# Key tiles on a fixed eight-tick cycle, log decays masked by GpSimd and exponentiated by ScalarE, gate steps one engine hop a tick

## Chip, cores and metric

The kernel runs on one core of a Trainium2 chip. The metric is the device time of one execution in microseconds, the median of several runs. A profile comes from one further execution. Engines: TensorE (PE; its weight loads are PEld), VectorE (DVE), ScalarE (ACT), GpSimd (POOL), and SyncE (SP), whose queue here issues DMAs only. Each engine works through its own queue in order and waits for the others by semaphores.

## The reference

One residual block on x of 1024 tokens by 1024 channels, all in float32. What matters here is the gated delta-rule branch (eight heads of 128 channels), which shares its input projection with a gated linear-attention branch and is followed by an output product and a squared-ReLU MLP.

```python
h = rms_norm(x, pre_mix_w) * (1.0 + scale1) + shift1        # scale1, shift1 from silu(c) @ ada_w
proj = h @ w_in                                             # d_qkv, d_beta, d_a and more are slices of it
d_qkv = silu(causal_short_conv(d_qkv, gdn_conv_w))          # four taps along the tokens
d_k = l2_norm(d_k)                                          # per token and head
beta = sigmoid(d_beta)
g = -exp(gdn_a_log) * softplus(d_a + gdn_dt_bias)
gc = cumsum(g)                                              # within a chunk of tokens
decay_mat = exp(where(causal, gc[:, None] - gc[None, :], -inf))
a_mat = where(strict, (k * beta) @ k.T * decay_mat, 0)
# then (a_mat + 1) is solved against the right-hand sides, and a scan over chunks follows
```

So for each head the key stage must give the keys, the sums of their squares, the decay matrices, and the products k k^T times the decay matrices.

## The kernel before

**Products in parts.** A float32 product is made of three passes in a reduced float32 format: each operand is split into a high part (hH, wH) and a rest (hL, wL). One dense product of 128 output channels for all 1024 tokens (`dense_b`, line 459) goes through eight contraction steps of six matmuls. After each step `tick()` advances a clock by one and runs what an agenda holds for it: `at(dt, fn)` (line 346) enters a function some ticks ahead, and `run_due` issues it behind the last matmul in TensorE's order. A tick decides only the place in the queues: VectorE, ScalarE, GpSimd and SP run their part as soon as their own queue and their inputs let them.

**Order.** `InOrder` (line 27) wraps an engine. While its flag `strict` is set, every instruction is placed behind the one before it on that engine, so the order is that of the program text and the agenda. The flag is set from line 135 to line 1333 (the end of the last key tile's dense product); from there a planner orders instructions by its own estimate and can also put later instructions between the strict ones where it thinks that an engine is free.

**Prologue** (lines 138 to 338). The tokens are loaded, squared (`x_sq`, ScalarE), scaled (`x_scale`, VectorE) and transposed in two groups (`x_tr` on TensorE, copied out of PSUM by `x_copy`). The conditioning vector's products are accumulated in four parts (`ada_pe`, `ada_out`), summed over partitions by `ada_fin` (TensorE) and turned into two columns per part, scale `am1` and shift `sh1`, by `ada_cols` (VectorE). `high(p)` makes two tiles of hH from the transposed tokens and these columns on ScalarE, `low(p)` the tiles of hL on VectorE.

**First tiles** (`first_tiles`, line 474). Two key heads and the 32 columns for low-rank gate, beta and a (weights `raw_lba`, split into `wS`) are computed together while the parts of the conditioning vector arrive. PSUM of a key head goes through `key_copy` (ScalarE: copy with the last tap), `key_tap` three times (VectorE), `key_tanh` (ScalarE) and `key_silu` (VectorE).

**Key stage** (lines 1312 to 1332). Tick 0 is the start of the first of six dense products, one for each of heads 2 to 7, which end at ticks 8, 16, ... 48. In their ticks run:

- the gates (`gates_small`, line 563): rows of beta and a go to DRAM and back into 64 partitions, then functions g6 to g11 at ticks 6 to 11 compute beta, the softplus, its running sum gc and derived columns. g8 writes gc to DRAM, g9 has GpSimd load it back, spread over 128 partitions, for heads 0 to 3 (`load_decay`, tile `Dk[h]`, named gr in the trace), g10 transposes three tiles on TensorE, g11 copies them to columns (gcC, betaC, ksC, beC);
- for each head `key_head` (line 709) with the ticks given in its call: transposes of the key in two halves, squares with sums (ktok), decays (eight instructions on VectorE per head: the row of gc less a column of gc, plus `negmask`, which is -1e30 above the diagonal), one exponential over the whole tile on ScalarE, Gram products in two halves on TensorE, their product with the decays (`times`, tile a0) on VectorE, and five stores. The tiles of gc have four buffers (tag hd), those of PSUM for these steps four (`pat`), and two for dense products (`pmt`).

For heads 4 to 7 the transposes stand at ticks 6 and 7 after the end of the head's dense product, and the silu at 5.

**After it** the agenda goes on during the two branch-gate products: `key_norms` (norms of the keys, two transposes of columns on TensorE), then `solve`, 64 steps on VectorE. `smask` is a mask tile that GpSimd fills at line 1345.

Of the kernel before, what the change touches and what calls it, by code (L numbers as in the profile page):

```python
# [50 lines left out]
def block_kernel(ctx: ExitStack, tc: tile.TileContext, x, c, ada_w, ada_b, pre_mix_w, post_mix_w,  # L51
# [253 lines left out]
    r1 = x_root(1)  # L305
    x_scale(1, r1)

# [166 lines left out]
    def first_tiles():  # L474
        wS = t4((128, 8, 64), F32R, "wS", "wt")
# [3 lines left out]
        A.copy(wS[:, :, 0:32], raw_lba)  # L479
        V.tensor_tensor(wS[:, :, 32:64], raw_lba, wS[:, :, 0:32].bitcast(F32), ALU.subtract)  # L480
# [61 lines left out]
        t1 = key_tanh(y1)  # L542
        key_silu(y1, t1)
# [13 lines left out]
    gcC = cp.tile([128, 64], F32, name="gcC")  # L557
# [5 lines left out]
    def gates_small(sb):  # L563
# [11 lines left out]
        def g6():  # L575
            A.activation(beta, bt, AF.Tanh, scale=0.5)
            V.tensor_scalar(beta, beta, 0.5, 0.5, ALU.mult, ALU.add)
            V.tensor_scalar(at_, at_, dtb, None, ALU.add)
            A.activation(e, at_, AF.Abs)
            A.activation(e, e, AF.Exp, scale=-1.0)  # L580
            A.activation(al, al, AF.Exp)

        def g7():
            V.tensor_scalar(u, e, 1.0, None, ALU.add)
            A.activation(l, u, AF.Ln)
            V.tensor_scalar(w, u, -1.0, None, ALU.add)
            V.tensor_tensor(w, e, w, ALU.subtract)
            V.reciprocal(u, u)
            V.tensor_mul(w, w, u)
# [30 lines left out]
        for i, fn in enumerate((g6, g7, g8, g9, g10, g11)):  # L620
            at(6 + i, fn)
# [15 lines left out]
        for t, fn in ((36, lr_high), (37, lr_low), (44, wlr_split)):  # L637
# [65 lines left out]
    Dk = {}  # L703
# [5 lines left out]
    def key_head(h, k, on, tr, decay, ex, gram):  # L709
# [1344 lines left out]
```

## Time and profile before

| | us |
|---|---|
| median of 3 runs | 1948.54 (1947.93 to 1952.42) |
| the profiled execution | 1951.02 |
| its span, first to last instruction | 1949.0 |
| TensorE busy in the span | 1910.4 |
| VectorE busy | 1343.5 |
| ScalarE busy | 811.4 |
| GpSimd busy | 141.4 |
| mean granted TensorE clock | 0.993 |

The profile gives a page of totals, groups of instructions, waits with what ended them, the chain of work that ended last, a timeline in order of time, and busy times in chosen stretches. Times in it are from the span's start. A row of the timeline reads: start, duration, engine, line, operation, output<-input, shapes, count, and in brackets the idle time before it and what ended it. All lines are L38, that of the helper that wraps the engines; tiles are told by name: cv is a key head between copy and silu, si a tanh, s the gates' tile, gr the decays, a the Gram products, wH and wL weight parts, pm and pa PSUM. The granted clock is that which TensorE's throttle let through, 1.00 being full.

### The profile page before, as it was taken

What the parts mean: (1) busy time and instruction counts of PE and PEld (TensorE: products, weight loads), DVE (VectorE), ACT (ScalarE), POOL (GpSimd) and SP (SyncE); (2) the same over time, 40 slices, a digit from 0 to 9 for tenths busy, and PEclk for the clock granted to TensorE, in tenths of its full rate; (3) what the DMA queues carried; (4) which work ended last, traced back from release to release, by engine and by line L of the source; (5) the groups of instructions that cost most, each with busy time, mean ns of one, the idle gap of its engine ahead of it and who ended that gap; (6) DMA issues with size and microseconds to landing.
All of it is one profiled execution on the core that took longest, in us unless ns stands there. A gap on an engine that the chain in (4) does not pass through costs nothing.

```text
span 1949.0 us, 25799 instructions
## 1 busy us (share of the span) xinstructions
PE 1910.4 (98%) x9873; PEld 1603.1 (82%) x9873; DVE 1343.5 (69%) x2427; ACT 811.4 (42%) x1477; POOL 141.4 (7%) x124
## 2 busy tenths in 40 slices
PE   6999999999999999999999999999999999999998
PEld 4687888889899888888887888888888888888886
DVE  5677699458768566766666244667578876787887
ACT  4545323342342334444445231357644446433333
POOL 1100100210101100000000110000012210000001
PEclk9999999999999999999999999999999999999999
DMA  9286423323122434444456986245656677452525
GB/s 326 71 254 208 140 98 111 127 66 109 53 78 66 142 107 137 128 129 129 129 190 162 226 191 145 87 130 167 219 197 229 226 237 267 143 205 74 196 97 98
DMA packets 213321, 296.96 MB, mean 152 GB/s; under 512 B 32687, under 2 KB 151710, under 8 KB 213198
## 3 DMA queue, kind: packets, MB, share of 16 engines
q1 hardware_dynamic: 188398, 259.38, 40.9%
q0 software_dynamic: 19280, 16.73, 5.5%
q10 hardware_dynamic: 5520, 19.21, 2.5%
q8 instruction: 77, 1.26, 0.3%
q14 instruction: 46, 0.38, 0.1%
HBM read 220.14 MB, written 75.15 MB: 152 GB/s over the span
## 4 chain that ended last, share of the span: by engine, by line
PE 91%; DMA 1%; DVE 1%; issue 1%; ACT 1%; POOL 0%; SPq 0%; DVEq 0%; POOLq 0%
PE pm L38 60%; PE pa L38 31%; DMA wL<-in_w_branch_gla_dram 1%; DVE cv L38 0%; ACT ktok L38 0%; DMA a_d<-a 0%; DVE gr L38 0%; ACT L38 0%; DVE ya L38 0%; DMA kt_d<-ktok 0%; DVE wL L38 0%; DVE lrS L38 0%; DVE rt L38 0%; ACT cv L38 0%; ACT wH L38 0%
## 5 line engine op out<-in xcount | busy, mean ns | idle before, releaser
L38 PE MATMUL pm<-hH,wH 128*128 128x512 f32 x992 | 327.2, 411 | 0.3 <-DVE cv L38 0.3
L38 PE MATMUL pm<-hL,wH 128*128 128x512 f32 x992 | 309.4, 393 | 0.0
L38 PE MATMUL pm<-hH,wL 128*128 128x512 f32 x992 | 308.0, 392 | 0.0
L38 PEld LDWEIGHTS pm<-hL,wH 128*128 128x128 f32 x992 | 187.2, 189 | 41.6
L38 PEld LDWEIGHTS pm<-hH,wL 128*128 128x128 f32 x992 | 187.0, 189 | 41.7
L38 PE MATMUL pa<-w,yH 128*128 128x512 f32 x688 | 212.0, 389 | 0.0
L38 ACT CAST wH<-raw 128x1024 fp32r<-128x1024 f32 x94 | 98.3, 1050 | 272.4 <-PE pm L38 197.4
L38 PEld LDWEIGHTS pm<-hH,wH 128*128 128x128 f32 x992 | 170.4, 191 | 22.6 <-issue 0.4
L38 DVE TENSOR_TENSOR w<-raw,w 128x512 fp32r<-128x512 f32 (+1 forms) x144 | 125.7, 877 | 49.1 <-ACT w L38 48.4
L38 PEld LDWEIGHTS pa<-w,yH 128*128 128x128 f32 x688 | 129.0, 188 | 27.3 <-DVE ya L38 0.4
L38 ACT CAST w<-raw 128x512 fp32r<-128x512 f32 (+1 forms) x142 | 97.2, 706 | 88.4 <-DVE raw L38 79.3
L38 PE MATMUL pa<-w,yL 128*128 128x512 f32 x344 | 133.8, 389 | 0.0
L38 PE MATMUL pa<-oB,w 128*128 128x512 f32 x480 | 111.4, 390 | 0.0
L38 DVE TENSOR_TENSOR wL<-raw,wH 128x1024 fp32r<-128x1024 f32 x78 | 94.7, 1218 | 22.0 <-ACT wH L38 11.9
L38 PEld LDWEIGHTS pa<-oB,w 128*128 128x128 f32 x480 | 89.7, 188 | 18.6 <-DVE w L38 0.2
L38 DVE SCALAR_TENSOR_TENSOR cv<-pm,ccol,cv 128x1023 f32<-128x1023 f32 (+2 forms) x72 | 92.0, 1277 | 13.9 <-ACT cv L38 12.9
L38 PE MATMUL pm<-oT,w 128*128 128x512 f32 x384 | 90.8, 389 | 0.0
L38 PE MATMUL pa<-oT,w 128*128 128x512 f32 x384 | 90.8, 389 | 0.0
L38 DVE TENSOR_TENSOR ya<-pa,ya 128x512 f32<-128x512 f32 x82 | 55.8, 688 | 43.7 <-PE pa L38 43.7
L38 PEld LDWEIGHTS pa<-oT,w 128*128 128x128 f32 x384 | 72.1, 188 | 15.0
L38 PEld LDWEIGHTS pm<-oT,w 128*128 128x128 f32 x384 | 72.1, 188 | 15.0
L38 PE MATMUL pm<-oH,wH 128*128 128x512 f32 x256 | 82.0, 402 | 0.9 <-DVE si L38 0.9
(339 smaller groups left out, 3665.4 us busy)
## 6 DMA issues: line engine op xcount, KB each, us to landing
yL<-y_d SPq DMA_DIRECT2D x53, 512.0 KB, 6.2
raw<-in_mlp_w_dram SPq DMA_DIRECT2D x23, 1024.0 KB
raw<-in_w_in_dram SPq DMA_DIRECT2D x20, 1024.0 KB, 7.4
raw<-in_w_in_dram SPq DMA_DIRECT2D x32, 512.0 KB, 4.1
araw<-in_ada_w_dram SPq DMA_DIRECT2D x32, 512.0 KB, 4.3
raw<-in_mlp_w_dram SPq DMA_DIRECT2D x18, 512.0 KB, 5.9
araw<-in_ada_w_dram SPq DMA_DIRECT2D x32, 256.0 KB, 6.8
sg_d<-sig ACTq DMA_DIRECT2D x16, 512.0 KB, 4.5
```

The source lines that it names most:

```text
L38: r = fn(*args, **kw)
```

## The change

In the prologue the split of the small weights `wS` moves from `first_tiles` to before and after the second `x_scale`; the conditioning sums of part 0 and their columns move between the transposes of the second group; one PSUM copy moves from ScalarE to VectorE. In `first_tiles` the tanh of head 0 is issued ahead of the copy of head 1, and the tanh and silu of head 1 go to ticks 2 and 3 of the key stage.

The gates' functions are cut anew, so that each holds about one engine's step after another's, and start at tick 3. The loads of gc for heads 0 to 3 are followed on GpSimd by `mask_decay`, which writes -1e30 above the diagonal of each tile; `negmask` goes. `decays` is now eight exponentials on ScalarE with the column of -gc (`gcN`, made by ScalarE from PSUM) as bias, in the place of eight instructions on VectorE and one exponential. `key_head` takes pairs of ticks for the two halves of each step, in a cycle of eight ticks from head 4 on: transposes at 9 and 13 after the dense product's end, squares a tick later, decays at 11 and 13, Gram products at 13 and 14, their products at 14 and 15.

```diff
     r1 = x_root(1)
+    wS = t4((128, 8, 64), F32R, "wS", "wt")
+    A.copy(wS[:, :, 0:32], raw_lba)
     x_scale(1, r1)
+    V.tensor_tensor(wS[:, :, 32:64], raw_lba, wS[:, :, 0:32].bitcast(F32), ALU.subtract)
...
     for i in range(4, 8):
+        if i == 6:
+            ada_fin(0)
+            ada_cols(0)
         x_tr(i, (4, 5, 0, 1, 2, 3) if i < 7 else (0, 1, 4, 5, 2, 3))
-    for d, E in ((0, A), (1, V), (4, A), (5, V), (2, A)):
+    for d, E in ((0, A), (1, V), (4, A), (5, V), (2, V)):
         x_copy(E, 1, d)
-    ada_fin(0)
-    ada_cols(0)
     banks[6:8] = [pat(), pat()]
     for i in range(4, 8):
         x_tr(i, (6, 7))
+    high(0)
     for d in (3, 6, 7):
         x_copy(V, 1, d)
-    high(0)
...
     def first_tiles():
-        wS = t4((128, 8, 64), F32R, "wS", "wt")
...
-        A.copy(wS[:, :, 0:32], raw_lba)
-        V.tensor_tensor(wS[:, :, 32:64], raw_lba, wS[:, :, 0:32].bitcast(F32), ALU.subtract)
...
-        y1 = key_copy(1, pk[1])
         for s_ in (1, 2, 3):
             key_tap(0, pk[0], y0, s_)
+        t0 = key_tanh(y0)
+        y1 = key_copy(1, pk[1])
         V.tensor_copy(sb[0:32], sb2[32:64])
         V.tensor_add(sb[0:32], sb[0:32], sb2[0:32])
-        t0 = key_tanh(y0)
         key_silu(y0, t0)
         for s_ in (1, 2, 3):
             key_tap(1, pk[1], y1, s_)
-        t1 = key_tanh(y1)
-        key_silu(y1, t1)
...
-        def g6():
+        def g3():
             A.activation(beta, bt, AF.Tanh, scale=0.5)
-            V.tensor_scalar(beta, beta, 0.5, 0.5, ALU.mult, ALU.add)
             V.tensor_scalar(at_, at_, dtb, None, ALU.add)
+
+        def g4():
             A.activation(e, at_, AF.Abs)
             A.activation(e, e, AF.Exp, scale=-1.0)
             A.activation(al, al, AF.Exp)
-
-        def g7():
+            V.tensor_scalar(beta, beta, 0.5, 0.5, ALU.mult, ALU.add)
+
+        def g5():
             V.tensor_scalar(u, e, 1.0, None, ALU.add)
-            A.activation(l, u, AF.Ln)
             V.tensor_scalar(w, u, -1.0, None, ALU.add)
             V.tensor_tensor(w, e, w, ALU.subtract)
-            V.reciprocal(u, u)
-            V.tensor_mul(w, w, u)
+
+        def g6():
+            A.activation(l, u, AF.Ln)
+            V.reciprocal(e, u)
+            V.tensor_mul(w, w, e)
...
         def g9():
+            for h in range(4):
+                load_decay(h)
+            for h in range(4):
+                mask_decay(h)
+
+        def g10():
             A.activation(kse, kse, AF.Exp)
             A.activation(dec, gc[:, 127:128], AF.Exp)
-            for h in range(4):
-                load_decay(h)
...
-            G.dma_start(decB, dec_d.partition_broadcast(128))
-
-        def g10():
+
+        def g12():
             z["ps"] = pat()
...
-        def g11():
-            for i, dst in ((1, gcC), (0, betaC), (2, ksC)):
+        def g13():
+            A.activation(gcN, z["ps"][:, 64:128], AF.Copy, scale=-1.0)
+            A.activation(beC, z["ps"][:, 64:128], AF.Exp)
+            for i, dst in ((0, betaC), (2, ksC)):
                 V.tensor_copy(dst, z["ps"][:, i * 64:(i + 1) * 64])
-            A.activation(beC, gcC, AF.Exp)
...
-        for i, fn in enumerate((g6, g7, g8, g9, g10, g11)):
-            at(6 + i, fn)
+        for t, fn in ((3, g3), (4, g4), (5, g5), (6, g6), (8, g8), (9, g9), (10, g10), (12, g12), (13, g13),
+                      (24, lambda: G.dma_start(decB, dec_d.partition_broadcast(128)))):
+            at(t, fn)
...
-        for t, fn in ((36, lr_high), (37, lr_low), (44, wlr_split)):
+        for t, fn in ((32, lr_high), (40, lr_low), (48, wlr_split)):
...
+    def mask_decay(h):
+        G.affine_select(out=r3(Dk[h]), in_=r3(Dk[h]), compare_op=ALU.is_ge, fill=-1e30, base=0,
+                        pattern=[[0, 8], [1, 128]], channel_multiplier=-1)
...
             for t in range(hf * 4, hf * 4 + 4):
-                V.scalar_tensor_tensor(gr[:, t * 128:(t + 1) * 128], gr[:, t * 128:(t + 1) * 128],
-                                       gcC[:, h * 8 + t:h * 8 + t + 1], negmask, ALU.subtract, ALU.add)
+                A.activation(gr[:, t * 128:(t + 1) * 128], gr[:, t * 128:(t + 1) * 128], AF.Exp,
+                             bias=gcN[:, h * 8 + t:h * 8 + t + 1])
...
-        on(tr, lambda: DMA.dma_start(kT_d[h], k))
-        on(tr, lambda: transposes(0))
-        on(tr + 1, lambda: squares(0))
-        on(tr + 1, lambda: transposes(1))
-        on(tr + (5 if h > 1 else 2), lambda: squares(1))
-        on(tr + 7, lambda: DMA.dma_start(kt_d[h], z["tok"]))
+        on(tr[0], lambda: DMA.dma_start(kT_d[h], k))
         for hf in range(2):
-            on(decay + hf, lambda hf=hf: decays(hf))
-            on(gram + hf, lambda hf=hf: grams(hf))
-            on(gram + hf + 1, lambda hf=hf: times(hf))
-        on(ex, lambda: A.activation(Dk[h], Dk[h], AF.Exp))
-        on(ex + 1, lambda: DMA.dma_start(Dt_d[h], Dk[h]))
-        on(gram + 3, spill)
+            on(tr[hf], lambda hf=hf: transposes(hf))
+            on(sq[hf], lambda hf=hf: squares(hf))
+            on(ex[hf], lambda hf=hf: decays(hf))
+            on(gram[hf], lambda hf=hf: grams(hf))
+            on(times_[hf], lambda hf=hf: times(hf))
+        on(sq[1] + 1, lambda: DMA.dma_start(kt_d[h], z["tok"]))
+        on(ex[1] + 1, lambda: DMA.dma_start(Dt_d[h], Dk[h]))
+        on(times_[1] + 1, spill)
         if h > 3:
-            on(decay - 6, lambda: load_decay(h))
+            on(ex[0] - 8, lambda: load_decay(h))
+            on(ex[0] - 3, lambda: mask_decay(h))
...
-    key_head(0, keys[0], on, 3, 13, 15, 17)
-    key_head(1, keys[1], on, 7, 15, 18, 19)
+    z1 = {}
+    on(2, lambda: z1.__setitem__("t", key_tanh(keys[1])))
+    on(3, lambda: key_silu(keys[1], z1["t"]))
+    key_head(0, keys[0], on, (1, 4), (3, 5), (19, 21), (21, 22), (22, 23))
+    key_head(1, keys[1], on, (6, 10), (7, 11), (23, 23), (23, 23), (24, 24))
...
-        key_head(h, y, on, e_ + 6, *{2: (20, 23, 25), 3: (23, 26, 30)}.get(h, (e_ + 6, e_ + 13, e_ + 14)))
+        ends = {2: ((27, 29), (29, 30), (30, 31)), 3: ((31, 31), (31, 31), (32, 32))}.get(
+            h, ((e_ + 11, e_ + 13), (e_ + 13, e_ + 14), (e_ + 14, e_ + 15)))
+        key_head(h, y, on, (e_ + 9, e_ + 13), (e_ + 10, e_ + 14), *ends)
...
-    at(14, key_norms)
-    at(26, lambda: next(sv))
-    due = 34.0
+    at(17, key_norms)
+    at(29, lambda: next(sv))
+    due = 37.0
```

More of the change, by code (lines that the diff above doesn't have):

```diff
@@ L556, in block_kernel @@
     nbrC = cp.tile([128, 64], F32, name="nbrC")
-    gcC = cp.tile([128, 64], F32, name="gcC")
+    gcN = cp.tile([128, 64], F32, name="gcN")
     ksC = cp.tile([128, 64], F32, name="ksC")
@@ L707, in load_decay, with key_head @@
         G.dma_start(Dk[h], gc_d[h].partition_broadcast(128))
-    def key_head(h, k, on, tr, decay, ex, gram):
+    def mask_decay(h):
+        G.affine_select(out=r3(Dk[h]), in_=r3(Dk[h]), compare_op=ALU.is_ge, fill=-1e30, base=0,
+                        pattern=[[0, 8], [1, 128]], channel_multiplier=-1)
+    def key_head(h, k, on, tr, sq, ex, gram, times_):
         z = {}
@@ L1299, in block_kernel @@
     cmask = cp.tile([128, 128], U32, name="cmask")
-    negmask = cp.tile([128, 128], F32, name="negmask")
     def masks():
@@ L1307, in masks @@
         G.tensor_copy(cmask, causal)
-        G.memset(negmask, 0.0)
-        G.affine_select(out=negmask, in_=negmask, compare_op=ALU.is_ge, fill=-1e30, base=0,
-                        pattern=[[1, 128]], channel_multiplier=-1)
     sb_lba, *keys = first_tiles()
```

## The prediction

> **What bounds the kernel now.** I read the totals, then TensorE's waits up to 250 us, then its busy time in stretches cut where a dense product begins or a wait ends, then the queues around each wait.
>
> ```profile
> span 1949.0 us, 25799 instructions
> PE 1910.4 (98%) x9873; PEld 1603.1 (82%) x9873; DVE 1343.5 (69%) x2427; ACT 811.4 (42%) x1477; POOL 141.4 (7%) x124
> ```
> ```profile
> PE pa L38 <- DVE cv L38: 4.9, 2, 4.0
> PE pa L38 <- DVE s L38: 2.7, 1, 2.7
> PE pm L38 <- ACT hH L38: 1.6, 1, 1.6
> PE pa L38 <- ACT s L38: 1.3, 1, 1.3
> PE pa L38 <- DVE wS L38: 0.7, 1, 0.7
> ```
> ```profile
> 88.20:105.10 16.90, 12.90 (x49) 0.80 0.93 266
> 105.10:121.50 16.40, 15.58 (x89) 1.00 0.85 229
> 121.50:136.90 15.40, 15.40 (x89) 1.00 0.83 275
> 136.90:156.30 19.40, 15.37 (x73) 0.91 0.61 190
> ...
> 27.26:30.67 3.41, 1.82 (x18) 1.00 1.09 347
> 30.67:34.09 3.42, 2.67 (x6) 0.50 1.10 349
> ...
> 116.00:119.40 3.40, 2.58 (x14) 1.00 1.00 344
> ```
>
> TensorE is the bound and is idle for 38.6 us in all. The waits that the edited code makes are the five quoted: 11.2 us. The columns of the stretches are length, TensorE busy, granted clock, DMA share, GB/s. A wait also costs afterwards: after the stretch that was busy for 1.82 of 3.41 us the clock is 0.50, and stays low for a whole further stretch in which matmuls run again. The short wait near 117 (2.58 busy of 3.40) left the clock at 1.00.
>
> The Trainium skill ("TensorE: Matmul & The Clock Gate", section "What's actually happening") says that TensorE's clock halves after an idle window of 3413 ns and returns after a busy one, the windows running free of the kernel. The trace agrees in length. By this rule the price of the same wait can differ between executions.
>
> The undisturbed stretch 121.5 to 136.9 holds one dense product (eight ticks), four halves of Gram products and two of transposes in 15.40 us. A tick is one contraction step, six matmuls, 1.36 us by those 15.40 less 0.90 for each Gram half and 0.46 for each transpose half. Against these prices:
> 88.2 to 105.1 (from the gates' transposes at tick 10 to the end of a dense product at tick 16: six ticks, two transpose halves, three small gate transposes of 0.3 in all: 9.4) loses **7.5**; 105.1 to 121.5 (the work of the undisturbed stretch) loses **1.0**; 136.9 to 156.3 (eight ticks, two Gram and two transpose halves: 13.6) loses **5.8**. Together 14.3 us.
>
> **The change, stage of the key tiles.** Times below are on the clock of the profile of before, as if the stage began where it did, at 72.40.
>
> ```profile
> 67.59 3.91 DVE L38 SCALAR_TENSOR_TENSOR cv<-pm,ccol,cv 128x1023 f32<-128x1023 f32 x3 [2.79 <-ACT cv L38]
> ...
> 72.25 1.21 DVE L38 TENSOR_TENSOR lba<-lba,lb 32x1024 f32<-32x1024 f32 x1
> ...
> 74.92 1.23 DVE L38 SCALAR_TENSOR_TENSOR cv<-si,cv 128x1024 f32<-128x1024 f32 x1 [1.45 <-ACT si L38]
> ...
> 77.08 0.52 POOL L38 DMA_DIRECT2D s<-ba_d  x1 [0.32 <-DMA ba_d<-lba]
> ...
> 86.81 1.28 ACT L38 ACT_TABLE_LOAD   x1
> ...
> 88.11 0.31 ACT L38 ACTIVATE s<-s 64x128 f32<-64x128 f32 x1
> ...
> 88.45 0.94 DVE L38 RECIPROCAL s<-s 64x128 f32<-64x128 f32 x1 [0.93 <-ACT s L38]
> ...
> 91.17 0.27 PE L38 MATMUL pa<-ident,s 64*128 64x64 f32 x1 [2.70 <-DVE s L38]
> ```
> ```profile
> DMA to landing us min/median/max: 1.8/3.8/4.6
> ```
> ```profile
> L38 ACT ACTIVATE ktok<-pa 128x128 f32<-128x128 f32 x64 | 16.7, 277 | 10.5 <-PE pa L38 6.2 <-POOL smask L38 4.3
> ```
>
> The landing times are those of the gates' tile s.
>
> *Head 0.* Its transposes move from tick 3 to tick 1. The tanh of head 0 now precedes the copy of head 1 on ScalarE, so it ends at 71.5 + 1.06 and no longer holds VectorE: the silu runs right behind the sum at 73.4 and ends at 74.65. Tick 1 is at 72.40 + 1.36 = 73.76, so TensorE waits there: a **new 0.9** (0 if the taps end earlier, 1.5 with one late hop).
>
> *Gates.* The steps start at tick 3 instead of 6, but their inputs are in SBUF only at about 77.08 + 3.8 = 80.9 (1.8 to 4.6: 78.9 to 81.7). VectorE's addition at tick 3 is queued ahead of the silu of head 1, which then ends at 82.3; its transposes are due at tick 6, at 82.4 (0 to 1 late, taken as 0.2). ScalarE goes on in order from 80.9: tanh, a half of head 0's squares (four of 0.277 and a copy, 1.7), absolute value and two exponentials to 83.5, the other half to 85.1, table load and logarithm to 86.7. Before, the transposes at 91.17 came 2.7 after the logarithm's end at 88.4; the reciprocal (0.94) is now done beside the table load, so VectorE's rest takes 1.7 from there, to 88.4. ScalarE meanwhile does a squares half, the copy of head 2 and a weight copy to 90.3, then table load and exponential (1.28 + 0.31) to 92.0. The three transposes are moved from tick 10 (88.2) to tick 12: 72.40 + 12 x 1.36 + four transpose halves 1.8 + the 1.1 above = 91.6. They wait **0.4**, with bounds 0 and 3; I take 0.6. That is less than the 0.8 us which left the clock at 1.00. So of 7.5 us some 1.7 come back.
>
> *Decays.* VectorE loses 64 instructions, ScalarE has 64 exponentials of 128x128 for 8 of 128x1024, GpSimd gets 8 masks of 128x1024.
>
> ```profile
> L38 DVE SCALAR_TENSOR_TENSOR gr<-gr,gcC,negmask 128x128 f32<-128x128 f32 x64 | 17.9, 343 | 4.5 <-DMA a_d<-a 2.5 <-DMA gr<-gc_d 2.0
> ...
> L38 ACT ACTIVATE gr<-gr 128x1024 f32<-128x1024 f32 x8 | 8.5, 1060 | 9.5 <-DVE gr L38 9.4
> ```
> ```profile
> 72.40:173.50 101.10, 91.97 (x459) 76.83 (x458) 73.72 (x131) 56.32 (x165) 9.30 (x17) 0.95 0.70 210
> ```
> ```profile
> 209.87 6.51 DVE L38 TENSOR_TENSOR X<-X,nb 128x1024 f32<-128x1024 f32 x4
> 211.22 7.27 POOL L38 TENSOR_SCALAR_AFFINE_SELECT X<-X 128x1024 f32<-128x1024 f32 x4 [59.90 <-DVE X L38]
> ...
> 344.80 5.50 POOL L38 TENSOR_SCALAR_AFFINE_SELECT X<-X 128x1024 f32<-128x1024 f32 x4 [126.32 <-DVE X L38]
> ```
>
> An exponential of 128x128 is nearest to the squares at 277 ns; from below, the eighth part of 1060, 133 ns. So ScalarE gets 0 to 9.2 us more on top of 56.3 in a stage of some 88: no bound. VectorE falls from 73.7 to 55.8. A mask costs 5.50 / 4 = 1.4 alone and 7.27 / 4 = 1.8 beside VectorE. The first four, with loads landing from about 94, run to about 101; the first exponential is due at tick 19, about 102. The write of the last decays and the load of head 4's now stand behind these masks on GpSimd; head 4's decays are wanted at tick 35, about 133, and that load can issue by 117. SP issues the same transfers per head, later. None of this is on TensorE's path as long as ScalarE keeps up; if it falls behind by over four ticks (5.4 us), transposes wait.
>
> *Why 136.9 to 156.3 lost 5.8.*
>
> ```profile
> 136.51 0.54 POOL L38 DMA_DIRECT2D gr<-gc_d  x1 [7.34 <-DVE a L38]
> ...
> 142.06 0.35 DVE L38 SCALAR_TENSOR_TENSOR gr<-gr,gcC,negmask 128x128 f32<-128x128 f32 x1 [2.50 <-DMA a_d<-a]
> ...
> 148.90 1.23 DVE L38 SCALAR_TENSOR_TENSOR cv<-si,cv 128x1024 f32<-128x1024 f32 x1
> ...
> 150.18 1.11 PE L38 MATMUL pa<-ident,cv 128*128 128x128 f32 x4 [4.04 <-DVE cv L38]
> ...
> 150.18 1.13 POOL L38 MEMSET smask<- 128x1024 f32 x2 [13.13 <-DVE cv L38]
> ```
>
> The load issued at 136.51 is the eighth, head 7's; its subtraction was put by the planner into VectorE's queue at 142.06, between two taps of head 5, and waited for the transfer. The taps, the split of the low-rank rows and the silu at 148.90 came late, and the transposes at 150.18 with them. That subtraction is gone from VectorE, and transposes now follow the silu by four ticks instead of one, which covers such a block. I take the 5.8 and the 1.0 as gone (bounds: half of them stays, or all go).
>
> *Key norms.* They move from tick 62 to 65, but head 7's second squares from 59 to 62, and the last products stand ahead of them on VectorE: transposes of the norms may wait 0 to 1; taken as 0.4. The solve starts three ticks later; it ends long before anything reads it, at 344.8.
>
> Sum of the stage: 14.3 - 0.9 - 0.2 - 0.6 - 0.4 = **12.2** (bounds 5 to 14).
>
> **The change, prologue.**
>
> ```profile
> 27.13 0.95 PE L38 MATMUL pa<-onesR,acc 128*128 128x1 f32 x8
> ...
> 28.72 0.15 DVE L38 TENSOR_TENSOR am<-pa,vcol 128x2 f32<-128x2 f32 x1
> ...
> 29.22 2.37 ACT L38 ACTIVATE hH<-xT,sh,am 128x1024 fp32r<-128x1024 f32 x2 [0.76 <-ACT xT L38]
> ...
> 37.35 1.23 DVE L38 TENSOR_TENSOR hL<-h,hH 128x1024 fp32r<-128x1024 f32 x1
> ...
> 40.87 1.17 PE L38 MATMUL pm<-hL,w 128*128 128x512 f32 x4
> ```
>
> The column sums at 27.13 move ahead of twelve transposes, so the columns (28.72) are there before 27.2 and the transposes end 0.8 later. ScalarE copies two banks instead of three and starts hH at 28.7 instead of 29.22; the first product comes at 30.1. The split of the small weight leaves 31.5 to 32.3, where TensorE waited 0.7, for idle time of ScalarE and VectorE. With no hole after 30.1 the stretch 30.67 to 34.09 is busy throughout, and the half clock should end one such stretch (3.4 us, worth 1.7) earlier. But VectorE's chain hardly moves: one more copy, no split of the small weight, so the last hL ends at 38.3 instead of 38.58. TensorE needed it at 41.3 and can at best have it at 38.4. Gain **2.6** (1.0 if the clock stays low, 3.0 by VectorE).
>
> Total 12.2 + 2.6 = 14.8. The profiled execution took 1951.0 with a span of 1949.0; its time becomes 1936.2. It stood 2.5 above the median of the runs, 1948.5, so **1934**.
>
> **The rivals.**
> *The gates' wait moves instead of going.* The chain of inputs, table load and logarithm is late by 3 more at tick 12 (inputs at 81.7, masks and loads on GpSimd in the way). Then 3.6 of waiting and a half clock of 6.8 us (3.4) appear: gain 14.8 - 6.4 = 8.4, time 1940. For it: four engines in a row with no slack at tick 12; against: the logarithm ends 1.7 us earlier than at 88.4, and its transposes stand two ticks later.
> *The change doesn't take the stalls away.* The planner may put exponentials of heads 6 and 7 into ScalarE's queue ahead of due work, as it did at 142.06 on VectorE, and the gates stay late too: only the prologue and some 1.5 remain, 1944.
> *Slower.* GpSimd waited 13.1 for a buffer at smask's memset (150.18). Say that the planner puts this memset ahead of head 7's mask, and that its buffer comes 5 us later since keys now live some four ticks longer. Then ScalarE's first exponential of head 7, and all behind it in order (squares, PSUM copies), blocks for 18.1 + 5.5 for the load (136.51 to 142.06) + 1.8 for the mask = 25.4. Free PSUM banks cover five ticks, 6.8; the other 18.6 and 3.4 for a low clock make 22.0, against 14.8: 1955.7. It decides from a block of 18.2. Against it: in the profile GpSimd's buffer waits cost TensorE nothing.
> *The port.* VectorE's four products of 6.51 took 1.6 each beside the masks of 7.27. The Trainium skill ("SBUF — State Buffer", section "SBUF: two separate sides") says that a GpSimd instruction and a VectorE one with two SBUF inputs exclude each other for a whole instruction. The trace agrees with a lock. Eight masks of at most 1.8 then hold VectorE by at most 14.4 us, less than the 17.9 it loses and each inside four ticks: this only feeds the first rival.
>
> **How the numbers follow.** Forecast 0.60 (1930 to 1938); moved wait 0.19 (1938 to 1942.7); no removal 0.14 (to 1953); slower 0.07 (1956). A change of 0.3% (5.8 us) is about what a measurement of this kernel can tell: faster 0.79, same 0.14, slower 0.07. The range: low 1930 (all 14.3 and 3.0 gone, and 1.3 for another clock phase), high 1944 (into the third case), leaving 2 in 10 out.
>
> **What would show it.** Right: no wait of TensorE for cv or s over 1 us between 72 and 195 of the old clock; one wait of some 0.9 one tick into the first dense product; granted clock 1.00 from the gates' transposes on; VectorE's busy time in the stage near 56, ScalarE's near 60; first hL product near 38.4. Wrong: a wait for ScalarE's s at the gates' transposes of over 1.5 us with a low clock behind it; transposes waiting for a silu behind a blocked ScalarE; TensorE holes after 195, where before has none until 657.

## The result and the profile after

The changed kernel takes 1937.36 us (median of 4 runs, 1935.93 to 1939.65) against 1949.97 us of the kernel before, measured beside it (4 runs, 1947.93 to 1952.42): ratio 0.993, 95% interval 0.9916 to 0.9944. It is faster by about 12.6 us.

Totals of the profile after, then TensorE's waits up to 250 us:

```profile
span 1937.7 us, 25813 instructions
PE 1903.6 (98%) x9873; PEld 1598.8 (83%) x9873; DVE 1327.4 (69%) x2363; ACT 821.6 (42%) x1533; POOL 149.0 (8%) x130
```
```profile
PE pa L38 <- DMA vt<-in_gdn_onorm_w_dram: 14.3, 1, 14.3
PE pa L38 <- DVE cv L38: 2.7, 3, 1.5
PE pm L38 <- DVE cv L38: 1.1, 1, 1.1
PE pm L38 <- DVE hL L38: 1.1, 1, 1.1
PE pm L38 <- ACT hH L38: 1.0, 1, 1.0
...
PE pa L38 <- DVE nbrC L38: 0.3, 1, 0.3
```

The waits of before for the gates' tile s (2.7 and 1.3) and for cv (4.0) are gone. What is left for keys (cv) is 3.8 us in four pieces.

To see where the 11.3 us of span went, I divided TensorE's time at four instructions that both programs have: its first instruction, the first dense product of the key stage, the first low-rank product (far behind the key stage), and the first product of the output stage. The columns of the stretches are as in the prediction; the number behind x is that of the matmuls. Before, then after:

```profile
12.99:72.62 59.63, 56.45 (x306) 39.36 (x307) 39.40 (x83) 25.21 (x39) 3.24 (x7) 0.94 0.66 216
72.62:339.82 267.20, 258.07 (x1213) 215.04 (x1211) 216.31 (x439) 106.70 (x230) 16.57 (x21) 0.98 0.50 159
339.82:1230.26 890.44, 886.08 (x5198) 761.65 (x5196) 549.94 (x1009) 335.94 (x687) 66.83 (x43) 1.00 0.45 127
```
```profile
14.30:72.81 58.51, 55.02 (x307) 39.74 (x307) 39.96 (x84) 25.43 (x37) 2.81 (x5) 1.00 0.66 212
72.81:330.83 258.02, 253.97 (x1213) 211.15 (x1211) 199.61 (x375) 116.37 (x287) 24.61 (x29) 1.00 0.53 169
330.83:1218.83 888.00, 884.79 (x5197) 760.69 (x5196) 549.94 (x1009) 336.26 (x687) 66.78 (x43) 1.00 0.45 127
```

I call the three the prologue, the key stretch and the middle. The first instruction came 1.3 later; the prologue took 1.1 less, the key stretch 9.2 less, the middle 2.4 less, the rest the same within 0.2: 11.4 less up to the output stage. In the key stretch, 5.1 of the 9.2 are idle time (9.13 before, 4.05 after) and 4.1 are busy time of the same 1213 matmuls: the half clock is gone. About the 2.4 of the middle the profiles show a wait for a weight of the output branch that lasted longer in before, with a half clock behind it (two matmuls in 1.22 against 0.73); e1 below shows that this varies without an edit. Before, then after:

```profile
1055.22 1.22 PE L38 MATMUL pm<-oH,wL 128*128 128x512 f32 x2 [1.97 <-DMA wL<-in_w_branch_gla_dram]
```
```profile
1045.14 0.73 PE L38 MATMUL pm<-oH,wL 128*128 128x512 f32 x2 [0.84 <-DMA wL<-in_w_branch_gla_dram]
```

The gates in the timeline after (VectorE's addition that waits for the tile s, ScalarE's logarithm and exponential, TensorE's transposes):

```profile
79.75 0.28 DVE L38 TENSOR_SCALAR s<-s,dtb 64x128 f32<-64x128 f32 x1 [1.13 <-DMA s<-ba_d]
...
85.17 0.31 ACT L38 ACTIVATE s<-s 64x128 f32<-64x128 f32 x1
...
90.38 0.31 ACT L38 ACTIVATE s<-s 64x128 f32<-64x128 f32 x1
...
91.91 0.40 PE L38 MATMUL pa<-ident,s 64*128 64x64 f32 x3
```

The exponential ends at 90.69, the transposes at tick 12 start at 91.91 and wait for nothing.

And the place where time is still lost, in the timeline after of GpSimd, ScalarE and TensorE:

```profile
125.57 0.71 POOL L38 DMA_DIRECT2D gr<-gc_d  x1
132.18 1.09 POOL L38 TENSOR_SCALAR_AFFINE_SELECT gr<-gr 128x1024 f32<-128x1024 f32 x1 [5.89 <-DMA gr<-gc_d]
133.22 0.55 POOL L38 DMA_DIRECT2D gr<-gc_d  x1
139.76 1.09 POOL L38 TENSOR_SCALAR_AFFINE_SELECT gr<-gr 128x1024 f32<-128x1024 f32 x1 [5.99 <-DMA gr<-gc_d]
140.81 0.55 POOL L38 DMA_DIRECT2D gr<-gc_d  x1
...
140.88 0.40 ACT L38 ACTIVATE gr<-gr,gcN 128x128 f32<-128x128 f32 x1 [8.80 <-POOL gr L38]
...
143.13 1.05 ACT L38 ACTIVATE si<-cv 128x1024 f32<-128x1024 f32 x1
...
145.49 0.66 PE L38 MATMUL pa<-ident,cv 128*128 128x128 f32 x4 [1.51 <-DVE cv L38]
...
159.11 0.70 PE L38 MATMUL pm<-hH,wH 128*128 128x512 f32 x2 [1.10 <-DVE cv L38]
...
161.37 0.66 PE L38 MATMUL pa<-ident,cv 128*128 128x128 f32 x4 [0.66 <-DVE cv L38]
```

ScalarE stood still for 8.80 us at an exponential of head 6, whose ticks lie behind the end of strict order, so that the planner put it ahead of work that was due, the tanh at 143.13 among it. It waited for GpSimd's mask, the mask for its load, and the load could issue only at 133.22, behind the mask of head 5, which had itself waited 5.89 for its own load. TensorE then waited 1.51, 1.10 and 0.66.

### The profile page after: what moved, and what is told of

It reads as the page before. It is cut to its first block, busy times and chain, and to the rows that moved or that the text cites. A ratio compares the mean times of both kernels' runs of the same rounds, so it can differ in the third digit from the quotient of the medians.

```text
span 1937.7 us, 25813 instructions
## 1 busy us (share of the span) xinstructions
PE 1903.6 (98%) x9873; PEld 1598.8 (83%) x9873; DVE 1327.4 (69%) x2363; ACT 821.6 (42%) x1533; POOL 149.0 (8%) x130
## 4 chain that ended last, share of the span: by engine, by line
PE 92%; DMA 3%; DVE 2%; issue 2%; ACT 1%; POOL 0%; SPq 0%; DVEq 0%; POOLq 0%; ACTq 0%
PE pm L38 60%; PE pa L38 31%; DMA wL<-in_w_branch_gla_dram 1%; DVE cv L38 1%; DMA Dt_d<-gr 1%; DMA a_d<-a 0%; DMA vt<-in_gdn_onorm_w_dram 0%; ACT gr L38 0%; DMA x<-in_x_dram 0%; DVE rt L38 0%; SPq L38 0%; POOL gr L38 0%; ACT xT L38 0%; DVE xT L38 0%; ACT si L38 0%
## 5 line engine op out<-in xcount | busy, mean ns | idle before, releaser
L38 PE MATMUL pm<-oH,wH 128*128 128x512 f32 x256 | 81.5, 400 | 0.9 <-DVE si L38 0.9
```

What stands on the lines that cost most here:

```text
L38: r = fn(*args, **kw)
```

## Experiments

The time of a run varies by 2 to 3 us either way (in e3 by up to 5.4), so parts are told apart by the stretches of their profiles, and the time only confirms. Most kernels have one profile; the changed kernel, which has two, differs between them by 2.1 us in the key stretch. All stretches, with each run's ratio to the kernel before that was measured beside it:

| kernel | prologue | key stretch | median, us | ratio (95%) |
|---|---|---|---|---|
| before | 59.6 | 267.2 | 1950.5 to 1952.1 in the later measurements | 1 |
| changed | 58.5 | 258.0 | 1937.36 | 0.993 (0.9916 to 0.9944) |
| e1 changed again | 58.7 | 255.9 | 1938.19 | 0.9931 (0.9916 to 0.9946) |
| e4 prologue only | 59.1 | 268.4 | 1949.92 | 0.9995 (0.9986 to 1.0004) |
| e5 gates only | 59.0 | 266.8 | 1949.95 | 0.9993 (0.9984 to 1.0003) |
| e7 decays only | 60.8 | 264.2 | 1948.97 | 0.9984 (0.9975 to 0.9994) |
| e8 cycle only | 59.4 | 257.2 | 1939.09 | 0.9940 (0.9925 to 0.9955) |
| e3 before, VectorE in order | 59.4 | 262.3 | 1944.54 | 0.9974 (0.9962 to 0.9986) |
| e6 gates, VectorE in order | 59.0 | 261.9 | 1944.00 | 0.9963 (0.9950 to 0.9976) |
| e2 changed, ScalarE in order | 58.6 | 253.7 | 1936.13 | 0.9923 (0.9907 to 0.9940) |
| e9 changed, decays back | 56.8 | 254.1 | 1935.80 | 0.9917 (0.9902 to 0.9932) |
| e10 | 58.8 | 253.0 | 1933.28 | 0.9902 (0.9886 to 0.9919) |
| e11 | 57.2 | 254.2 | 1935.22 | 0.9915 (0.9901 to 0.9930) |
| e12 | 56.8 | 253.0 | 1934.71 | 0.9915 (0.9901 to 0.9928) |

In e10 and e12 TensorE has no idle time in the key stretch at all, so its floor is 253.0; before lost 14.2 there.

### What varies without an edit: e1

The changed kernel, unedited.

> The changed kernel once more, for a second profile. In the first one its span was 11.3 us shorter than before's: of this 9.15 lay between the first dense product and the gated attention, 2.4 near 1045 us (a wait for a weight of the branch output, 1.97 against 0.84, and a half clock behind it in before alone), and the prologue gave -0.2 because TensorE's first instruction came at 14.30 instead of 12.99 and its first group of transposes ran at half clock. Theory: only the 9.15 belongs to the change, so this profile has again 9.0 to 9.3 there, while the first instruction (12.9 to 14.4), the clock in the first transposes and the wait near 1045 may fall either way. Rival: all three belong to the change and come out as they did (14.3, half clock, 0.84). Time 1937.4, within 2.

```profile
18.27 1.12 PE L38 MATMUL pa<-ident,x 128*128 128x128 f32 x4 [0.83 <-DVE x L38]
...
156.29 0.70 PE L38 MATMUL pm<-hH,wH 128*128 128x512 f32 x2 [0.67 <-DVE cv L38]
...
158.55 0.66 PE L38 MATMUL pa<-ident,cv 128*128 128x128 f32 x4 [0.64 <-DVE cv L38]
```

The key stretch gained not 9.2 but 11.3, out of the range I gave: ScalarE was blocked for 6.63 instead of 8.80, the wait of 1.51 is gone, and the other two are 0.67 and 0.64. The middle took 890.0 (888.0 in the first profile), so its 2.4 were not the change's; over all profiles of this study the middle lies between 886.9 and 890.4. The first instruction came at 13.47, but the first transposes are at half clock again (1.12 for four; before 0.66).

### The blocked queue, before and after: e3 and e2

e3 is the kernel before with VectorE's order kept longer, e2 the changed kernel with ScalarE's:

```diff
     for e in strict:
-        e.strict = False
+        e.strict = e is V                               # e2: e is A
+    at(16, lambda: setattr(V, "strict", False))         # e2: at(17, ...), A
```

> The kernel before with one edit: VectorE keeps to the order of the program for 16 ticks longer, so that head 7's subtractions cannot stand between the taps of head 5. Nothing of the change is in it. The prediction put the 5.8 us lost from 136.9 to 156.3 down to this subtraction at 142.06, waiting for its load. Theory: the wait of 4.04 and the low clock behind it go, 5.8 less than before (at least 2.9), about 1944. Rival: the transposes stand only one tick behind the silu, and the row of work on VectorE is late anyway; then the wait moves to another instruction and less than 1.5 is gained.

> The changed kernel with one edit: ScalarE keeps to the order of the program for 17 ticks longer, so that the planner cannot put the exponentials of heads 6 and 7 ahead of due work. In the changed kernel's profile ScalarE stood still for 8.80 us until 140.88 at head 6's first exponential, which waited for GpSimd's mask, and TensorE then waited 1.51, 1.10 and 0.66 us (3.3 in all) for keys that ScalarE served late. Theory: that order is the cause; the three waits go, 1934 (3.3 less than the changed kernel in the same call). Rival: ScalarE has simply too much to do there (busy for 15.6 of 20 us); then waits of over 2 us stay at other places and the time is that of the changed kernel within 1.

The transposes that waited 4.04 in before, in e3:

```profile
146.76 0.66 PE L38 MATMUL pa<-ident,cv 128*128 128x128 f32 x4 [1.17 <-DVE cv L38]
```

Of the 5.8, 4.9 came back in the key stretch and 6.1 in the median time (95% interval 2.7 to 7.4), from an edit of the order alone that changes no instruction. The cause named in the prediction holds: with head 7's subtraction out of its place between the taps, the long wait is gone and no half clock follows (0.66 for the four transposes). A wait of 1.17 is left where the transposes stand one tick behind the silu. Two of e3's nine runs took 1949.9; the profile is of the fastest, so what those two lost isn't known.

In e2 the three waits are gone, and up to 250 us TensorE waits for keys once:

```profile
PE pa L38 <- DVE cv L38: 0.5, 1, 0.5
```

The key stretch is 253.7, 4.3 and 2.2 less than in the two profiles of the changed kernel, the median time 2.1 less than e1's, measured beside it, which the runs don't tell apart (their ratios' intervals overlap). ScalarE does not have too much to do; its order was at fault.

### The parts of the change alone: e4, e5, e7, e8

e4 is the kernel before with the diff's prologue edits alone.

> The kernel before with the edits of the prologue alone (split of the small weights, sums and columns of part 0, one PSUM copy, order of hH). The prediction gave them 2.6 us (1.0 to 3.0). In the profiles from TensorE's first instruction to the first dense product: 59.6 us before, 58.5 in the changed kernel, in which the first transposes ran at half clock for 3.5 us. Theory: a gain of 1.1 with that half clock and of 2.8 without it, so 56.8 to 58.5 for this stretch and 1.1 to 2.8 of the time. Rival: the gain is lost again at VectorE's second hL, and the stretch stays at 59.6 within 0.3, with no gain in the time.

```profile
17.88 1.11 PE L38 MATMUL pa<-ident,x 128*128 128x128 f32 x4 [0.83 <-DVE x L38]
...
40.78 0.72 PE L38 MATMUL pm<-hL,w 128*128 128x512 f32 x2 [1.06 <-DVE hL L38]
```

The prologue took 59.05, between the theory's 56.8 to 58.5 and the rival's 59.3 to 59.9; the time did not move clear of noise (0.7 less, interval from 2.7 less to 0.8 more). The first transposes ran at half clock, as in the changed kernel. With 16 warm-up transposes they did so in 5 of 11 profiles, among them one without the prologue edits (e7: 60.8). Like is compared with like: at half clock 60.8 without the edits (one profile) and 58.5 to 59.1 with them (four, mean 58.7), so 2.1; at full clock 59.0 to 59.6 without (five, mean 59.3) and 56.8 with them (e9), so 2.4. By these comparisons, each with a single profile on one side, the edits are worth about what was predicted, and a half clock in the first transposes, worth about 2, can hide it. One rival stays open: the half clock came in 4 of 5 profiles with the edits and in 1 of 6 without them, which is too few to say whether the edits make it more likely.

e5 is the kernel before with the gates' functions of the change (g3 to g13, without masks; gcC copied on VectorE).

> The kernel before with the gates' steps alone as in the change (from tick 3, transposes at tick 12); the decays stay subtractions on VectorE, the ticks of the heads and the prologue as before. From the first dense product to the first low-rank product (TensorE) the profiles have 267.2 us before and 268.4 with the prologue edits alone. Theory (the prediction's 7.5 us that become 0.6): the waits of 2.7 and 1.3 at the gates' transposes and the low clock behind them go, the stretch is 260 to 262, the time 6 to 7 less than before, 1944. Rival: the chain of input, logarithm and running sum has no slack at tick 12 without the rest of the change; then a wait of over 1.5 at those transposes with a low clock stays and less than 2 is gained.

```profile
93.20 1.28 ACT L38 ACT_TABLE_LOAD   x1
94.50 0.31 ACT L38 ACTIVATE s<-s 64x128 f32<-64x128 f32 x1
...
94.86 0.27 PE L38 MATMUL pa<-ident,s 64*128 64x64 f32 x1 [3.88 <-ACT s L38]
```

The rival holds: 2.7 and 1.3 became one 3.88, and the key stretch gained 0.4. In the old ticks the second halves of head 1's squares and a weight copy stand on ScalarE ahead of the second table load, and the exponential comes at 94.50 instead of 90.38.

e7 is the kernel before with exponentials on ScalarE, `gcN` and masks on GpSimd, at the old ticks (load at decay - 6, mask at decay - 1).

> The kernel before with the decays alone as in the change (exponentials with the column as bias on ScalarE, masks on GpSimd), at the old ticks. In this program's order five exponentials of head 7 stand on ScalarE ahead of the tanh of head 5, where before the subtraction of head 7 stood among VectorE's taps. Theory: the block only changes its engine, and waits for the mask (1.1 to 1.8) behind the same load: the transposes of head 5 wait 4 to 6 with a low clock behind, the stretch from the first dense product to the first low-rank product is 266 to 270 against 267.2, the time that of before within 3. Rival (the step of the prediction): what leaves VectorE's queue is gone, the stretch is 261 to 263, the time 5 to 6 less.

```profile
147.12 1.57 ACT L38 ACTIVATE gr<-gr,gcN 128x128 f32<-128x128 f32 x5 [4.91 <-POOL gr L38]
148.60 1.04 ACT L38 ACTIVATE si<-cv 128x1024 f32<-128x1024 f32 x1
...
150.95 0.66 PE L38 MATMUL pa<-ident,cv 128*128 128x128 f32 x4 [3.43 <-DVE cv L38]
```

Neither number was right (264.2). The mechanism is the one of the theory: the block changed its engine, and the transposes of head 5 still wait, 3.43 instead of 4.04. The 3.0 that the stretch gained are these 0.6, the wait of 0.8 near 117 that is gone, and a half clock that did not follow (full clock after 150.95; a half-speed stretch of 3.4 us, worth 1.7, in before).

e8 is the kernel before with the ticks of `key_head` and its calls, those of the key norms and the solve, and the places of the first two heads' tanh and silu as in the change, the decays still on VectorE (subtractions, then one exponential per half).

> The kernel before with the ticks of the heads alone as in the change (transposes at 9 and 13 behind the product's end, the other steps of the eight-tick cycle, the tanh of head 0 ahead of the copy of head 1); decays on VectorE, gates' steps and prologue as before. Head 7's subtraction can still be put early into VectorE's queue. Theory: four ticks between silu and transposes cover that block, so the wait of 4.0 at head 5's transposes is gone or under 1; the gates' waits of 2.7 and 1.3 stay; the stretch from the first dense product to the first low-rank product is 261 to 264, the time 4 to 6 less than before. Rival: the blocked taps hold the PSUM of the next product, so the wait moves from the transposes to the products and less than 2 is gained.

TensorE's waits from 72 to 250 us:

```profile
PE pa L38 <- ACT s L38: 1.3, 1, 1.3
PE pa L38 <- DVE cv L38: 0.5, 1, 0.5
PE pa L38 <- DVE nbrC L38: 0.3, 1, 0.3
```

This alone is about the changed kernel's time: 257.2 and 1939.09. It did more than the theory said (261 to 264): the long waits for cv went, and the gates' two waits became one of 1.3, with the old gates' steps. ScalarE shows why, in its tanh of head 1 and the tanh of the gates. Before, then e8:

```profile
80.05 1.06 ACT L38 ACTIVATE si<-cv 128x1024 f32<-128x1024 f32 x1 [5.17 <-issue]
...
85.26 0.31 ACT L38 ACTIVATE s<-s 64x128 f32<-64x128 f32 x1
```
```profile
78.59 1.06 ACT L38 ACTIVATE si<-cv 128x1024 f32<-128x1024 f32 x1 [3.58 <-issue]
...
82.85 0.31 ACT L38 ACTIVATE s<-s 64x128 f32<-64x128 f32 x1
```

Head 0's tanh runs ahead of head 1's copy, so VectorE's taps and head 1's tanh come 1.5 earlier; and a weight copy that stood behind that tanh (81.02) now runs in idle time ahead of it (73.97). ScalarE reaches the gates 2.4 earlier, with the same two halves of head 0's squares ahead of them.

### Two parts together: e6

e5's gates with e3's order of VectorE.

> The kernel before with two things only: the gates' steps of the change, and VectorE kept in the order of the program for 16 ticks longer (which by itself took the stretch from the first dense product to the first low-rank product from 267.2 to 262.3 and the time from 1950.6 to 1944.5). Decays, masks, ticks of the heads and prologue are as before. Theory: gates and order are the two causes, and moving the decays to ScalarE and GpSimd and the eight-tick cycle give nothing more: the stretch is 254.5 to 257, as in the changed kernel (258.0 and 255.9) or less, the time 1938 within 2. Rival: decays and cycle each carry a share; then this stays at 259 or more, 1941 or more.

The rival holds: 261.9 against e3's 262.3. Without the cycle the gates' steps add 0.5 and wait 3.91.

### One part taken back: e9

The changed kernel with `decays` on VectorE and `mask_decay` gone.

> The changed kernel with the decays alone put back: subtractions with the mask on VectorE, one exponential per half on ScalarE, no masks on GpSimd, at the ticks of the change; gates' steps, cycle and prologue of the change stay. From the first dense product to the first low-rank product the changed kernel took 258.0 and 255.9, the cycle alone 257.2, the changed kernel with ScalarE in order 253.7. Theory: the move of the decays gives nothing in this cycle, and gave the planner ScalarE's queue to put blocked exponentials into; with the decays back the stretch is 253.5 to 256, no wait of over 0.7 stands between the gates' transposes and the key norms, and the time is 1936 to 1938, not above the changed kernel's 1938. Rival: VectorE, relieved by 18 us in this stage, needs the relief; then waits for cv of 1 to 4 us appear, the stretch is 258 to 262, the time over 1940.

The loads of gc for heads 6 and 7 on GpSimd, and TensorE's first transposes:

```profile
125.34 0.54 POOL L38 DMA_DIRECT2D gr<-gc_d  x1 [8.20 <-DVE gr L38]
132.22 0.54 POOL L38 DMA_DIRECT2D gr<-gc_d  x1 [6.35 <-DMA Dt_d<-gr]
...
19.40 0.66 PE L38 MATMUL pa<-ident,x 128*128 128x128 f32 x4 [0.83 <-DVE x L38]
```

The theory holds: 254.1, and only waits of 0.52 and 0.25 in the stretch. Without masks in GpSimd's queue the two loads issue 7.9 and 8.6 us earlier than in the changed kernel (133.22 and 140.81), or 6.5 and 7.2 counted from each key stretch's start. So no subtraction waits for them, although the planner may still move subtractions ahead. VectorE is busy for 81.5 of 101 us there and does not need the relief. Against e8 (257.2) the stretch is 3.2 shorter: 1.3 of idle time, the gates' wait, and 1.9 of busy time of the same matmuls, the half clock. So the gates' steps are worth 0.4 alone and 3.2 with the cycle, as far as one profile each can tell; e9 also has the prologue's edits, which lie ahead of this stretch.

### Versions for what is left: e10, e11, e12

e10 is e2 with three edits; e11 has the same three, with the decays back on VectorE and both queues in order; e12 is e10 without the split.

```diff
-    key_head(0, keys[0], on, (1, 4), (3, 5), ...
+    key_head(0, keys[0], on, (2, 4), (3, 5), ...
-    WARM = 16
+    WARM = 20
     ada_out(0)
+    # e10, e11: wk made here, wk_low(0) here and wk_low(1) behind ada_cols(0), instead of in first_tiles
```

> The changed kernel with ScalarE kept in order for 17 ticks (253.7 from the first dense product to the first low-rank product), and three edits for the waits that are left: head 0's transposes at tick 2 (a wait of 0.52 at tick 1), the split of the first two heads' weights moved into VectorE's idle time ahead of the second group's copies (a wait of 1.06 for the second hL), and 20 instead of 16 warm-up transposes (0.83 idle ahead of the first group, and half clock for 3.4 us in it). Theory: each wait goes and none takes its place, 1.06 + 0.52 and up to 1.2 of half clock: the stretch to the first dense product (58.6 from TensorE's first instruction) is 56 to 57.5, the next 253.0 to 253.4, the time 1933 to 1935. Rival: the wait for hL only turns into one of TensorE's own work (no gain to the first dense product beyond 0.5), 1936, as with ScalarE in order alone.

> As the run with the decays put back on VectorE, with VectorE and ScalarE both kept in order for 17 ticks, and the three edits of the run beside it (transposes of head 0 at tick 2, earlier split of the first weights, 20 warm-up transposes). Theory: with both queues in order it does not matter which engine makes the decays, as both have idle time: the same time as the run beside it within 1 us (1933 to 1935), the stretch from the first dense product to the first low-rank product within 0.5 of its. Rival: the eight ticks are too short for VectorE with the decays on it (busy 73.7 of 101 us before, 55.8 without them), and waits for cv or for the key norms of 1 us and more make it slower by 1 to 4.

> The fastest kernel so far (1933.3: the changed kernel with ScalarE in order for 17 ticks, head 0's transposes at tick 2, 20 warm-up transposes, earlier split of the first weights) without the earlier split. With it VectorE waited 2.61 for GpSimd's copy of the weights at 27.92, its first split took 2.03 beside that copy, the columns of part 0 came late and TensorE waited 1.84 at 30.43 with a half clock behind it: 58.8 from TensorE's first instruction to the first dense product, against 56.8 in the run with the decays put back, which had the prologue of the change and a full clock in its first transposes. Theory: without the split the wait of 1.84 goes, the one of 1.06 for the second hL comes back, and the 20 transposes keep the full clock: 56.5 to 57.2 for that stretch, 252.9 to 253.3 for the next, 1931 to 1933. Rival: the half clock is no matter of that wait or of the warm-up and comes back at the first transposes; then the stretch is 58.5 and the time 1933 to 1935.

e10, VectorE and TensorE:

```profile
27.92 2.03 DVE L38 TENSOR_TENSOR w<-raw,w 128x1024 fp32r<-128x1024 f32 x1 [2.61 <-POOL w L38]
...
30.43 0.96 PE L38 MATMUL pa<-ident,x 128*128 128x128 f32 x7 [1.84 <-DVE sh L38]
```

The key stretch is at its floor. The earlier split was a mistake: VectorE waited in order for GpSimd's copy, the columns of part 0 came late, and TensorE waited 1.84, with a half clock behind it. e11 missed its forecasts (within 1 of e10's time, within 0.5 of its stretch): it took 1.9 and 1.25 more, the rival's numbers, but not for the rival's cause. The new wait is one that the prediction had named: the gates' addition waited 3.05 for its input at 80.83, the silu of head 1 behind it, and head 1's transposes 1.03. The first decays come after it, so their engine has no part in it.

e12:

```profile
18.57 0.66 PE L38 MATMUL pa<-ident,x 128*128 128x128 f32 x4 [0.62 <-DVE x L38]
...
39.25 0.73 PE L38 MATMUL pm<-hL,w 128*128 128x512 f32 x2 [1.05 <-DVE hL L38]
```

Both stretches came as forecast (56.8 and 253.0). Its median, 1934.71, is above the range given, though its profiled execution took 1932.2; e9 to e12 lie within 2.5 us of each other, and their times do not rank them. Each lies below the changed kernel's two medians, by 1.6 to 4.9 us, with intervals that still overlap its own.

## Why the prediction was right, and where not

The time, 1937.4, lies in the range and in the interval of the likeliest case (1930 to 1938), 3.4 above the forecast.

- **What was lost before:** right. Against the 14.3 us of the three stretches stand 14.2 of the whole key stretch by the floor found later; of its 9.13 idle, 8.85 lie between 88.2 and 156.3.
- **Head 0 at tick 1:** predicted 0.9, measured 0.52 and 0.51. **Head 1 at tick 6:** predicted 0.2 (0 to 1), measured 0, and 1.03 in e11, by the mechanism named. **Key norms:** 0.4 against 0.26.
- **Gates:** predicted 0.6, measured 0; the inputs came at 79.75 (80.9 said), the logarithm ended at 85.5 (86.7), the exponential at 90.7 (92.0). What the prediction missed is that this depends on the cycle: it listed ScalarE's squares between the gates' steps, but credited the gates' own steps. By e5, e8 and e9 the steps alone bring 0.4, the cycle alone leaves a wait of 1.3, and both together leave none. It also left out that the earlier tanh of head 1 and the weight copy ahead of it give ScalarE 2.4 us (e8).
- **The 5.8 from 136.9 to 156.3:** the cause is right (e3). The step "I take the 5.8 and the 1.0 as gone" is not: 3.3 of waits came back in the first profile and 1.3 in the second, inside its bounds (half of them stays). That is the second rival, planner and ScalarE, at a part of its price. The prediction kept it apart as a rival, but it happened inside the forecast's case, and one of its own signs of being wrong, transposes behind a silu behind a blocked ScalarE, came true while the time came out right. Its step on the decays failed in one place: it counted the write of the last decays and head 4's load behind the masks, but not that in GpSimd's order each later load stands behind the mask of the head before, which waits for its own load. Load, 6 us and mask make 7.6 us for each head (125.57, 133.22, 140.81).
- **Decays:** VectorE was relieved as said, but the relief was worth nothing in this cycle (e9). An exponential cost 0.31 (eight in 2.46 us), above the bound of 0.277; a mask 1.1, below the 1.4 taken. The busy times that were to show it (VectorE near 56, ScalarE near 60) are not what a stretch of the old length has:

```profile
72.81:173.91 101.10, 97.31 (x509) 81.36 (x508) 65.33 (x73) 68.86 (x225) 18.27 (x25) 1.00 0.71 219
```

  It holds 509 matmuls where before's held 459: the stage runs faster, so more of the work behind it falls inside. Those two numbers should have been given for equal work, not for equal time.
- **Prologue:** 2.6 predicted, 0.7 in the time (e4, within its uncertainty), 2.1 and 2.4 like with like. The mechanism was right: the first hL product came 25.4 after TensorE's first instruction (27.9 before; 23.7 in e9, at full clock), the columns came earlier, the half clock after 30 is gone, and TensorE now waits 1.07 for VectorE's second hL, the limit that was named. What failed is the unsaid step that the first transposes run at the clock that they had in one profile. Whether the edits change that clock is open.
- **Minus 2.5 for the profiled execution:** wrong. It rested on three runs; the later medians of before, of 7 to 20 runs each, are 1950.5 to 1952.1, so that its 1951.0 was an ordinary run. Without that step the forecast would have been 1936.2, within 1.2 of the result.

On the scale of the profiles the forecast was 1936.2 and the profiled execution took 1939.65. The difference of 3.45 is 3.0 (12.2 against 9.2 in the key stretch) and 2.8 (2.6 against -0.2 in the prologue with its later start), less the 2.4 of the middle, which no step counted and which is luck.

The slower rival did not come: smask's memset stood behind head 7's mask. The port that VectorE and GpSimd share held VectorE at single instructions only (last section). Which part carried the change is another answer than the prediction's: the eight-tick cycle brings 10.0 of the key stretch alone, the gates' steps 3.2 on top of it, and moving the decays costs 1.8 to 4.0 unless ScalarE is kept in order.

## What to carry to other kernels

When a stall goes back to an instruction that a planner put early into an in-order queue, look for what would go into the same place after the change: work moved to an idle engine takes the block with it, and here keeping one queue in order was worth 4.9 us of the stretch by itself before the change. If loads and the work that waits for them share a queue, each load waits for the one before it to land. Take the parts of a change singly and then in pairs: the gates' steps were worth 0.4 alone and 3.2 with the cycle.

## What the runs showed of the hardware

**The clock of the first transposes can differ between executions.** With the same 16 warm-up transposes and 0.8 to 1.2 us idle behind them, the next four took 0.66 in six profiles and 1.11 or 1.12 in five; this costs about 2 us. e2 and e9 have the same program up to there and the same idle time of 0.83, and took 1.11 and 0.66. With 20 warm-up transposes they took 0.66 to 0.67 in three of three; three are too few to call it settled. The Trainium skill ("TensorE: Matmul & The Clock Gate", section "What's actually happening") says that the window which releases the clock runs free of the kernel, so that its phase decides. The traces agree in that the clock differs where the program doesn't; none shows the phase.

**GpSimd's masks and VectorE.** In the changed kernel, a mask and a weight product that began beside it:

```profile
102.64 1.09 POOL L38 TENSOR_SCALAR_AFFINE_SELECT gr<-gr 128x1024 f32<-128x1024 f32 x1 [1.40 <-DMA gr<-gc_d]
...
103.01 1.79 DVE L38 TENSOR_TENSOR wL<-raw,wH 128x1024 fp32r<-128x1024 f32 x1
```

The same product takes 1.21 to 1.22 elsewhere. It lasted 0.6 longer, about what was left of the mask when it began (103.73 less 103.01). The Trainium skill ("SBUF — State Buffer", section "SBUF: two separate sides") calls the port pair that the two engines share an exclusive lock, held for a whole instruction. The trace agrees, and the price here is about the remainder of the mask. e1 and e2 have one such piece each around the fourth mask: a silu of 2.03 instead of 1.22, and the mask itself 1.95 and 1.87 instead of 1.09.
